# A hybrid encoder layer on one core: the last 256 gate and up columns as one unit of seven block products, S5's chain paced anew, and an idle product ahead of the keys

## The chip, the cores and the metric

The kernel runs on one core of a Trainium2 chip. The metric is the time of one execution on the device in microseconds, as a median of several runs. Beside it stands one profiled execution, with its own time and a trace of every instruction.

## The reference

The layer takes 512 tokens of width 1024 in float32. Cut to what matters:

```python
n = rms_norm(h, mix_norm_g)
proj = n @ w_in                                   # 1024 -> 512 + 4 * 1024
xa, zu, zv = ...                                  # S5 input, gating inputs
gate_a, gate_b = sigmoid(...), sigmoid(...)
ya = s5_branch(xa, ...)                           # two diagonal recurrences, forward and backward, GLU
yb = gelu(zu) * (w_s @ layer_norm(gelu(zv)) + bias)   # 128-token chunks, 8 heads
h = h + (gate_a * (ya @ w_proj_a) + gate_b * (yb @ w_proj_b)) @ w_out
h = h + cross_attention(rms_norm(h), rms_norm(mem))   # 256 memory tokens, 4 heads
f = rms_norm(h, ffn_norm_g)
h = h + (silu(f @ w_gate) * (f @ w_up)) @ w_down      # 1024 -> 2816 -> 1024
return rms_norm(h, final_norm_g)
```

## The kernel before, in words

Every large product keeps nearly the accuracy of float32: an operand is split into a high part (a cast on ScalarE, line 85) and a remainder (a subtraction on VectorE, line 86), and a product is three matmuls, high x high, high x low, low x high (`mm3`). TensorE reads the parts, so each weight block of 512 KB costs a load, a cast and a subtraction. `plan` lists all weight blocks in the order of their use; `next_w` issues the loads of the next ones and splits the next two (`SPLITS`); the parts rotate through three buffers, `hi` and `lo`.

The queries, the gate and up products and the down product save one product in eight: with both operands cut into 2 x 2 blocks, seven products of sums of blocks stand for the eight (Strassen's scheme in Winograd's form). A **unit** is 512 columns of a gate or up matrix. Its seven products are numbered 1 to 7; each takes a weight block `b11`, `b21`, `b22` or a sum `t` of blocks, against a block of the token matrix `fn` or a sum of such blocks (`ops`). The tokens are cut into T0 and T1 (256 each), the 1024 rows into K0 and K1. Products 1 and 2 need only T0; product 5 needs the first token sum (`sum1`: T1 rows of K0 minus T1 rows of K1), 6 and 7 the next ones (`sum2`), 3 the last (`sum4`). A product is 24 matmuls of 256 columns (`product`, line 1331). The block sums of the weights are made by an adding DMA on GpSimd's queue (line 181) and by VectorE (line 184). The pool `stp[0]` holds two buffers each of `t`, `b21` and `b22`; `b11` lies in the three raw buffers.

The inner width is 2816 = 5 x 512 + 256. The ten units (gate and up, five times 512 columns) are followed by the down product. The last 256 columns of gate and up (from `FS` = 2560 on) are plain products, four blocks of gate and four of up, which run first, with products 1 and 2 of unit 0 between the gate blocks. Under them the last token tile's norm, its transposes and the token sums are made. `begun` holds the started next unit; each unit's loop runs 5, 6, then 1 of the next unit, 7, 2 of the next unit, 4, 3. `put` writes the activation: SiLU for gate, a multiplication for up. `pair` holds the result of the last 256 columns.

`long_idle` is a matmul of 512 columns whose result nobody reads. Two stand in the kernel: behind the last token tile's transposes ahead of the feed-forward part (`behind=ot_hi`), and behind product 5 of unit 0.

Ahead of this runs the mixing stage. The S5 branch is a side program, a Python generator that `tick` drives while the large products run: `tick(us)` gives it `us * side["rate"]` of credit, and each `yield` takes some. `later(n, f)` calls `f` after n steps, a step being 5.2 us of ticks. Per octet of groups `s5_kernels` makes the factors `e` on VectorE, the block-diagonal tiles `bd` (two memsets on GpSimd, four copies on ScalarE), the products `pk`, and then stores, spills to DRAM and loads the kernels `tt` (16 small DMAs on GpSimd's queue). `pump` applies one ready set of input weights per half step (`pz`). `s5_scan` is the recurrence on VectorE, four small instructions a step. `s5_outputs` mixes (`py`), applies gelu (`squash`), turns back (`back`, `pyt`) and writes out. The gating loop (`psv`, line 1092) evacuates eight heads on VectorE (line 1093).

The order of each engine's instructions is settled when the program is built, from program order and a model of durations, as `schedule_with_timeline_sim=True` says; only instructions marked `in_order` keep theirs. So the trace's order is not always that of the text.

Of the kernel before, what the change touches and what calls it, by code (L numbers as in the profile page):

```python
# [17 lines left out]
P = 128  # L18
# [34 lines left out]
def hybrid_layer_kernel(  # L53
# [108 lines left out]
    def plan_unit(w, c0, ordered=False):  # L162

        kh = KD // 2
        b = lambda i, j: block(w, i * kh, kh, c0 + 256 * j, 256)
        r = {}

        def fresh(nm):
            r[nm] = (wp if nm == "b11" else stp[0]).tile([P, kh, 256], F32, tag="raw" if nm == "b11" else nm,
                                                         name=nm, bufs=3 if nm == "b11" else 2)  # L170
            return r[nm]

        def plain(nm, src):
            def f():
                ins = nc.sync.dma_start(fresh(nm), src)
                if ordered:
                    in_order(ins)
            return f

        def onto(nm, src):  # L180
            return lambda: nc.gpsimd.dma_start(r[nm], src, accum_op=ALU.add)

        def tt(o, x, y, op):
            nc.vector.tensor_tensor(r[o], r[x], r[y], op)
# [38 lines left out]
    def plan_units(units, down):  # L223


        made = [plan_unit(*u, ordered=i == 1) for i, u in enumerate(units)]
        for i in range(2):
            plan_block(w_gate, 4 * i, 4, FS, 256, place=i + 1)
            plan.append(made[0][i + 1])
        plan_feat(w_up, FS, KD)  # L230
        for i, m in enumerate(made):
            nx = made[i + 1] if i + 1 < len(made) else {}
            between = [nx[1]] if nx else down[:2]
            plan.extend([m[5], m[6]] + between + [m[7]] + ([nx[2]] if nx else []) + [m[4], m[3]])
        plan.extend(down[2:])
# [76 lines left out]
    FS = 2560  # L312
    UNITS = [(w, c0) for c0 in range(0, FS, 512) for w in (w_gate, w_up)]
    down_tokens, down_plan = [], []
# [454 lines left out]
    def s5_kernels(o):  # L769
# [3 lines left out]
        pr, pi = st["pe"]  # L773
        es = []
        for i in range(2):
# [12 lines left out]
        def products():  # L788
            bd = []
            for i in range(2):  # L790
                t = s5p.tile([P, GO, 2, C], F32, tag="bd", name="bd", bufs=2)
                nc.gpsimd.memset(t, 0.0)
                for d in range(2):
                    hf = slice(64 * d, 64 * d + 64)
                    nc.scalar.copy(t[hf, :, d, :], st["b"][i][hf, gs, :])
                bd.append(t)
            ps = aux("pk", (P, 2, P))
# [16 lines left out]
        def store(ps):  # L814
# [5 lines left out]
            V.tensor_tensor(ks[:, :, 0:C], ks[:, :, 0:C], dd, ALU.add)  # L820
            later(1, lambda: spill(ks))

        def spill(ks):
            kd = dp.tile([GO, C, 15, C], F32, name=f"kd{o}")
            for j in range(4):
                kdj = kd.rearrange("(q j) c l e -> j c q (l e)", j=4)[j]
                nc.gpsimd.dma_start(kdj[:, :, 7 * C:15 * C], ks[32 * j:32 * j + C])
                nc.gpsimd.dma_start(kdj[:, :, 0:7 * C], ks[32 * j + C:32 * j + 2 * C, :, 0:7 * C])
            later(2, lambda: load(kd))

# [41 lines left out]
    def pump():  # L872
        if "u" in st and ready:
            n, wt = ready.pop(0)
            apply(*SETS[n], wt)
            applied.append(n)
        if len(applied) < len(SETS):
            later(0.5, pump)
# [25 lines left out]
    def s5_outputs(o):  # L904
# [28 lines left out]
        def squash(ps):  # L933

            nc.scalar.activation(yt[:, 0], ps, AF.Gelu_apprx_tanh)
            later(0.5, back)

# [147 lines left out]


    gbc = gbcs[0]
    sv = slot("A", (P, H, T), F32, "sv")
    for h in range(H):
# [6 lines left out]
        tick(0.9)  # L1096

    yb_hi = slot("E", (P, KD, T), F32R, "yb_hi")
    yb_lo = slot("D", (P, KD, T), F32R, "yb_lo")
# [122 lines left out]
    for half in range(2):  # L1222
        tokm(w_out, half * 512, mg, KD, add_evac(half, 0, feat_norm(g_x, hn_hi, hn_lo, hfull, True)))

# [230 lines left out]

    def gate_evac(m, j, ps):
        nc.scalar.activation(pair[:, j, :], ps, AF.Silu)

    def up_evac(m, j, ps):
        nc.vector.tensor_tensor(pair[:, j, :], pair[:, j, :], ps, ALU.mult)  # L1460


    a11, a12, a21, a22 = full[:, K0, T0], full[:, K1, T0], full[:, K0, T1], full[:, K1, T1]
# [20 lines left out]

    def unit_start(u):
        x, v = unit_bank("px"), unit_bank("pv")
        product(x, u, 1, True, ops)
        nc.scalar.copy(v, x)
        return x, v

    def put(u, f, ts, src):
        dst = acts(u[1] // 512, f)[:, :, ts]
        if u[0] is w_gate:
# [9 lines left out]

    ps = [bank("pf0"), bank("pf1")]
    ws = []

    def gate_part(i, ts):
        if ts is T0:
            ws.append((4 * i,) + next_w(w_gate, 4 * i, 4, FS, 256))
        feat_block(ps, ws[i], fn, KD, 4, ts, ts is T0)  # L1510
        tick(2.7)

    gate_part(0, T0)
    begun = unit_start(UNITS[0])
    gate_part(1, T0)
    unit_second(UNITS[0], begun[1])
    for i in range(2):
        gate_part(i, T1)
    for j in range(2):
        gate_evac(FS // P + j, j, ps[j])  # L1520
    sum1()
    later(1, sum2)
    feat(w_up, FS, fn, KD, up_evac, parts=2, ps=[aux("pf0"), aux("pf1")])
    V.tensor_tensor(pair[:, 0, T1], pair[:, 0, T1], pair[:, 1, T1], ALU.subtract)

# [44 lines left out]
    for i, u in enumerate(UNITS):  # L1570
        final = i == len(UNITS) - 1
        x, v = begun
        q = unit_bank("pq")
# [10 lines left out]
        nc.scalar.copy(u2, x)  # L1584
        if not final:
            begun = unit_start(UNITS[i + 1])
        else:
# [6 lines left out]
        if not final:  # L1594
# [141 lines left out]
```

## Time and profile before

| | us |
|---|---|
| median of 3 runs | 887.28 (887.0 to 889.22) |
| profiled execution | 885.71 |
| its span, first to last instruction | 883.9 |
| TensorE busy | 867.2 |
| VectorE busy | 623.7 |
| ScalarE busy | 477.8 |
| GpSimd busy | 99.6 |

The page's shares are shares of the span. PE is TensorE, PEld its weight loads, DVE VectorE, ACT ScalarE, POOL GpSimd, SPq the queue of the engine that issues most loads. The chain of waits gives start, length and what the time went to; a timeline row gives start, length, engine, line, operation, output and inputs, and in brackets the idle time ahead of it with what ended it. The mean granted clock of TensorE is 0.997.

### The profile page before, as it was taken

The page shows a single profiled execution, that of the slowest core. Times are in us where ns is not written, and L with a number is a line of the kernel's source. Part 1 is how long each engine was busy: PE and PEld are TensorE (multiplying, and loading weights), DVE is VectorE, ACT ScalarE, POOL GpSimd, SP SyncE. Part 2 cuts the span into 40 slices and gives each one's busy share as a digit, 9 for nine tenths or more (in the row PEclk, how much of TensorE's full clock was granted, in tenths as well). Part 3 has the DMA queues.
Part 4 walks back from the last instruction along what each step waited for, and adds up shares of the span by engine and source line. Part 5 has one row for each costly group of instructions (what it writes and reads, how often), then busy time and mean ns, then how long its engine had stood idle before and what let it go on. Part 6 is the DMA issues. An engine that isn't in the chain of part 4 may idle for free.

```text
span 883.9 us, 14489 instructions
## 1 busy us (share of the span) xinstructions
PE 867.2 (98%) x5625; PEld 765.1 (87%) x5625; DVE 623.7 (71%) x1020; ACT 477.8 (54%) x702; POOL 99.6 (11%) x162
## 2 busy tenths in 40 slices
PE   9999999999989999999999999999999999999996
PEld 6788888888768888889899878999999999888875
DVE  5699718997542367659757746767877768899875
ACT  6644887245754343548556535545445555556663
POOL 1001045100063010110000001101110110000000
PEclk9999999999999999999999999999999999999999
DMA  9449368975278777925678235536799963256672
GB/s 267 140 108 260 86 167 221 252 183 142 64 182 230 197 237 195 289 84 166 204 226 253 72 102 157 147 101 174 193 216 211 232 164 95 72 168 202 191 246 87
DMA packets 112134, 154.33 MB, mean 175 GB/s; under 512 B 13545, under 2 KB 78593, under 8 KB 112002
## 3 DMA queue, kind: packets, MB, share of 16 engines
q1 hardware_dynamic: 93042, 128.27, 45.8%
q0 software_dynamic: 16432, 24.09, 16.9%
q10 hardware_dynamic: 2592, 1.05, 0.5%
q8 instruction: 44, 0.72, 0.3%
q14 instruction: 24, 0.20, 0.1%
HBM read 146.60 MB, written 38.24 MB: 209 GB/s over the span
## 4 chain that ended last, share of the span: by engine, by line
PE 86%; ACT 5%; DVE 4%; DMA 3%; issue 2%; SPq 1%; POOLq 0%; POOL 0%; ACTq 0%; DVEq 0%
PE pf L350 24%; PE pt L350 16%; PE px L1331 12%; PE dx L350 7%; PE pq L1331 6%; PE dq L350 3%; PE pv L1331 3%; PE qx L1331 2%; PE dv L350 2%; PE po L350 1%; PE qq L1331 1%; DMA xt<-in_x_dram 1%; PE ptr L511 1%; PE pz L884 1%; ACT ss L916 1%
## 5 line engine op out<-in xcount | busy, mean ns | idle before, releaser
L86 DVE TENSOR_TENSOR wlo<-wraw,whi 128x1024 fp32r<-128x1024 f32 (+1 forms) x139 | 165.0, 1187 | 103.3 <-ACT whi L85 98.0
L85 ACT CAST whi<-wraw 128x1024 fp32r<-128x1024 f32 (+1 forms) x139 | 142.3, 1024 | 157.0 <-PE pf L350 43.0
L350 PE MATMUL pf<-xn,whi 128*128 128x512 f32 x448 | 139.9, 392 | 0.0
L350 PEld LDWEIGHTS pf<-xn,whi 128*128 128x128 f32 x448 | 83.5, 188 | 17.4 <-issue 0.5
L350 PE MATMUL pf<-xn,wlo 128*128 128x512 f32 x224 | 87.6, 391 | 0.0
L1331 PE MATMUL px<-fn,whi 128*128 128x256 f32 x480 | 83.3, 276 | 0.0
L1331 PEld LDWEIGHTS px<-fn,whi 128*128 128x128 f32 x480 | 72.4, 188 | 0.3 <-ACT u L1591 0.2
L85 ACT CAST whi<-b 128x1024 fp32r<-128x1024 f32 x40 | 42.1, 1054 | 50.3 <-PE px L1331 27.1
L86 DVE TENSOR_TENSOR wlo<-b,whi 128x1024 fp32r<-128x1024 f32 x40 | 48.9, 1223 | 27.1 <-ACT whi L85 27.1
L1331 PE MATMUL px<-fn,wlo 128*128 128x256 f32 x240 | 66.4, 277 | 0.0
L350 PE MATMUL dx<-whi,s 128*128 128x512 f32 x170 | 53.9, 392 | 1.4 <-ACT whi L85 1.0
L1331 PE MATMUL pq<-s,whi 128*128 128x256 f32 x320 | 55.1, 276 | 0.0
L85 ACT CAST whi<-t 128x1024 fp32r<-128x1024 f32 x30 | 31.6, 1054 | 36.1 <-PE pv L1331 12.9
L86 DVE TENSOR_TENSOR wlo<-t,whi 128x1024 fp32r<-128x1024 f32 x30 | 36.7, 1225 | 19.9 <-ACT whi L85 19.9
L350 PEld LDWEIGHTS pf<-xn,wlo 128*128 128x128 f32 x224 | 42.1, 188 | 8.9 <-issue 0.2
L1331 PEld LDWEIGHTS pq<-s,whi 128*128 128x128 f32 x320 | 48.2, 188 | 0.1
L1331 PEld LDWEIGHTS px<-fn,wlo 128*128 128x128 f32 x240 | 45.1, 188 | 0.0
L1331 PE MATMUL pq<-s,wlo 128*128 128x256 f32 x160 | 44.2, 277 | 0.0
L350 PE MATMUL pt<-whi,xn 128*128 128x512 f32 x128 | 42.7, 407 | 0.0
L350 PEld LDWEIGHTS dx<-whi,s 128*128 128x128 f32 x170 | 31.7, 188 | 8.5 <-ACT whi L85 1.2
L350 PE MATMUL dx<-wlo,s 128*128 128x512 f32 x85 | 33.2, 391 | 0.0
L1331 PEld LDWEIGHTS pq<-s,wlo 128*128 128x128 f32 x160 | 30.1, 188 | 0.0
(422 smaller groups left out, 2159.8 us busy)
## 6 DMA issues: line engine op xcount, KB each, us to landing
wraw<-in_w_in_dram SPq DMA_DIRECT2D x36, 512.0 KB, 5.0
dsum<-in_w_down_dram SPq DMA_DIRECT2D x20, 512.0 KB, 6.7
wraw<-dsum SPq DMA_DIRECT2D x20, 512.0 KB, 3.7
b<-in_w_gate_dram SPq DMA_DIRECT2D x15, 512.0 KB, 3.9
b<-in_w_up_dram SPq DMA_DIRECT2D x15, 512.0 KB, 5.4
wraw<-in_w_down_dram SPq DMA_DIRECT2D x15, 512.0 KB, 3.9
dsum<-in_w_down_dram POOLq DMA_DIRECT2D x10, 512.0 KB, 7.3
dsum<-dsum POOLq DMA_DIRECT2D x10, 512.0 KB, 7.2
```

Source lines behind the costliest of these rows:

```text
L85: hi = nc.scalar.copy(dst_hi, src)
L86: lo = nc.vector.tensor_tensor(dst_lo, src, dst_hi.bitcast(F32), ALU.subtract)
L350: nc.tensor.matmul(ps, a[x], b[y], start=start and i == 0, stop=stop and i == 2, skip_group_check=free)
L511: tr = nc.tensor.transpose(ps[:, j, :], src[:, k * P:(k + 1) * P], ident)
L884: nc.tensor.matmul(ps[:, g, :], wt[:, g, :], st["u"][:, o * GO + g, :], start=True, stop=True)
L916: nc.scalar.copy(s[lo_, :, 1:NCH], zv[lo_, :, 0:NCH - 1])
L1331: nc.tensor.matmul(ps[:, j, :], a[x], b[y], start=start and j == k == i == 0, stop=k == 3 and i == 2, skip_group_check=True)
```

## The change

1. The last 256 columns of gate and up become one unit of seven products, with gate as the first block column and up as the second. It is the first of eleven units. The eight plain products and their evacuations go.
2. Products 1 and 2 of the first two units and product 1 of the third are run ahead of the loop; product 2 of the third stands between products 6 and 7 of the first. `sum1` and `sum2` follow directly, not a step apart. From the third unit on, the loop is as before.
3. In S5, the `bd` tiles are made ahead of the factors `e` instead of with the products; the spill comes after half a step and the load after one (one and two before); the turn back one step after the gelu (half before); `pump` applies up to two sets at a time; during the gating loop the side program's rate is 0.3 instead of 0.8.
4. The transposes of the last token tile ahead of the attention keep program order, and an idle product on `mg_hi` follows them.

```diff
@@ plan_unit
-        b = lambda i, j: block(w, i * kh, kh, c0 + 256 * j, 256)
+        b = (lambda i, j: block((w_gate, w_up)[j], i * kh, kh, FS, 256)) if c0 == FS else \
+            lambda i, j: block(w, i * kh, kh, c0 + 256 * j, 256)
@@ plan_units
-        for i in range(2):
-            plan_block(w_gate, 4 * i, 4, FS, 256, place=i + 1)
-            plan.append(made[0][i + 1])
-        plan_feat(w_up, FS, KD)
+        plan.extend([made[i][q] for i in range(2) for q in (1, 2)] + [made[2][1]])
...
-            plan.extend([m[5], m[6]] + between + [m[7]] + ([nx[2]] if nx else []) + [m[4], m[3]])
+            if i < 2:
+                plan.extend([m[5], m[6]] + ([made[2][2]] if i == 0 else []) + [m[7], m[4], m[3]])
+            else:
+                plan.extend([m[5], m[6]] + between + [m[7]] + ([nx[2]] if nx else []) + [m[4], m[3]])
...
-    UNITS = [(w, c0) for c0 in range(0, FS, 512) for w in (w_gate, w_up)]
+    UNITS = [(w_gate, FS)] + [(w, c0) for c0 in range(0, FS, 512) for w in (w_gate, w_up)]
@@ s5_kernels: the loop that makes bd moves from products() to the start
-            later(1, lambda: spill(ks))
+            later(0.5, lambda: spill(ks))
-            later(2, lambda: load(kd))
+            later(1, lambda: load(kd))
@@ pump
-        if "u" in st and ready:
-            n, wt = ready.pop(0)
...
+        for _ in range(2):
+            if "u" in st and ready:
...
@@ squash
-            later(0.5, back)
+            later(1, back)
@@ the gating loop
+    side["rate"] = 0.3
...
+    side["rate"] = RATE
@@ w_out
-        tokm(w_out, half * 512, mg, KD, add_evac(half, 0, feat_norm(g_x, hn_hi, hn_lo, hfull, True)))
+        tokm(w_out, half * 512, mg, KD, add_evac(half, 0, feat_norm(g_x, hn_hi, hn_lo, hfull, True, behind=mg_hi)))
@@ put
+        if u[1] == FS:
+            dst = pair[:, :, ts]
+            if f == 0 and ts is T0:
+                nc.scalar.activation(dst, src, AF.Silu)
+            else:
+                if f == 0:
+                    t = np_.tile([P, 2, 256], F32, tag="ev", name="gate", bufs=2)
+                    nc.scalar.activation(t, src, AF.Silu)
+                    src = t
+                nc.vector.tensor_tensor(dst, dst, src, ALU.mult)
+            return
@@ ahead of the loop
-    gate_part(0, T0)
-    begun = unit_start(UNITS[0])
-    gate_part(1, T0)
-    unit_second(UNITS[0], begun[1])
...
-    sum1()
-    later(1, sum2)
-    feat(w_up, FS, fn, KD, up_evac, parts=2, ps=[aux("pf0"), aux("pf1")])
-    V.tensor_tensor(pair[:, 0, T1], pair[:, 0, T1], pair[:, 1, T1], ALU.subtract)
+    starts = []
+    for u in UNITS[:2]:
+        starts.append(unit_start(u))
+        unit_second(u, starts[-1][1])
+    starts.append(unit_start(UNITS[2], lambda name: aux(name, (P, 2, 256))))
+    sum1()
+    sum2()
@@ the loop over units
-        x, v = begun
+        x, v = begun if i > 2 else starts[i]
...
+        if i == 0:
+            unit_second(UNITS[2], starts[2][1])
...
-        V.tensor_tensor(u3, q, u3, ALU.subtract)
-        put(u, 1, T1, u3)
+        if i == 0:
+            V.tensor_tensor(pair[:, :, T1], q, u3, ALU.subtract)
+        else:
+            V.tensor_tensor(u3, q, u3, ALU.subtract)
+            put(u, 1, T1, u3)
...
+        elif i == 0:
+            V.tensor_tensor(pair[:, 0, T1], pair[:, 0, T1], pair[:, 1, T1], ALU.subtract)
```

More of the change, by code (lines that the diff above doesn't have):

```diff
@@ L773, in s5_kernels @@
         pr, pi = st["pe"]
-        es = []
+        es, bd = [], []
+        for i in range(2):
+            t = s5p.tile([P, GO, 2, C], F32, tag="bd", name="bd", bufs=2)
+            nc.gpsimd.memset(t, 0.0)
+            for d in range(2):
+                hf = slice(64 * d, 64 * d + 64)
+                nc.scalar.copy(t[hf, :, d, :], st["b"][i][hf, gs, :])
+            bd.append(t)
         for i in range(2):
@@ L788, in products @@
         def products():
[L789 to L796, printed above, removed]
             ps = aux("pk", (P, 2, P))
@@ L872, in pump @@
     def pump():
-        if "u" in st and ready:
-            n, wt = ready.pop(0)
-            apply(*SETS[n], wt)
-            applied.append(n)
+        for _ in range(2):
+            if "u" in st and ready:
+                n, wt = ready.pop(0)
+                apply(*SETS[n], wt)
+                applied.append(n)
         if len(applied) < len(SETS):
@@ L1454, in acts @@
         return rest[0][:, 2 * f:2 * f + 2, :]
[L1456 to L1460, printed above, removed]
     a11, a12, a21, a22 = full[:, K0, T0], full[:, K1, T0], full[:, K0, T1], full[:, K1, T1]
@@ L1483, in hybrid_layer_kernel, with unit_start @@
     ops = {1: fn_q(K0, T0), 2: fn_q(K1, T0), 7: fn_q(K0, T1), 4: fn_q(K1, T1)}
-    def unit_start(u):
-        x, v = unit_bank("px"), unit_bank("pv")
+    def unit_start(u, place=unit_bank):
+        x, v = place("px"), place("pv")
         product(x, u, 1, True, ops)
@@ L1500, in unit_second @@
         put(u, 0, T0, v)
[L1504 to L1511, printed above, removed]
-    gate_part(0, T0)
-    begun = unit_start(UNITS[0])
-    gate_part(1, T0)
-    unit_second(UNITS[0], begun[1])
[L1517 to L1520, printed above, removed]
+    starts = []
[3 more added lines that the diff above has]
+    starts.append(unit_start(UNITS[2], lambda name: aux(name, (P, 2, 256))))
     sum1()
-    later(1, sum2)
-    feat(w_up, FS, fn, KD, up_evac, parts=2, ps=[aux("pf0"), aux("pf1")])
-    V.tensor_tensor(pair[:, 0, T1], pair[:, 0, T1], pair[:, 1, T1], ALU.subtract)
+    sum2()
     made, last_job = {}, []
@@ L1584, in hybrid_layer_kernel @@
         nc.scalar.copy(u2, x)
-        if not final:
+        if 1 < i and not final:
             begun = unit_start(UNITS[i + 1])
-        else:
+        elif final:
             dx = [bank(f"dx{t}") for t in range(2)]
             down_product(dx, 1, True, range(2))
+        if i == 0:
+            unit_second(UNITS[2], starts[2][1])
         product(x, u, 7, False, ops)
@@ L1593, in hybrid_layer_kernel @@
             sum4()
-        if not final:
+        if 1 < i and not final:
             unit_second(UNITS[i + 1], begun[1])
-        V.tensor_tensor(u3, q, u3, ALU.subtract)
-        put(u, 1, T1, u3)
+        if i == 0:
[3 more added lines that the diff above has]
+            put(u, 1, T1, u3)
         product(x, u, 4, False, ops)
```

## The prediction

> **What bounds the kernel now.** I read the page's busy shares and its chain by engine first, then the chain of waits of the stretches that the change touches.
>
> ```profile
> span 883.9 us, 14489 instructions
> ...
> PE 867.2 (98%) x5625; PEld 765.1 (87%) x5625; DVE 623.7 (71%) x1020; ACT 477.8 (54%) x702; POOL 99.6 (11%) x162
> ...
> PE 86%; ACT 5%; DVE 4%; DMA 3%; issue 2%; SPq 1%; POOLq 0%; POOL 0%; ACTq 0%; DVEq 0%
> ```
>
> TensorE carries 86% of the chain that ends last, so there are only two ways to save time: fewer or shorter products, or fewer moments in which TensorE waits. The waits of PE, as who waited for whom, show how little there is of the second kind; these three lie in the S5 and gating stretch:
>
> ```profile
> PE pk L802 <- DVE e L785: 1.6, 1, 1.6
> PE pyt L941 <- ACT tt L935: 1.1, 1, 1.1
> ...
> PE psv L1092 <- DVE sv L1093: 0.9, 1, 0.9
> ```
>
> The chain, cut to the start of the feed-forward part, gives the price of a block product (24 matmuls of 256 columns):
>
> ```profile
> 564.51 0.23 PE long L503
> ...
> 566.86 16.96 PE pf L350 x144
> 583.82 2.83 PE pq L1331 x24
> 586.65 0.23 PE long L503
> ...
> 595.06 2.72 PE pv L1331 x24
> ```
>
> Two prices stand here: 16.96/6 = 2.83 us before the idle product at 586.65, and 2.72 us behind it. TensorE streams without a break in both. Why it has two paces the trace does not say; I only count with them.
>
> **Part 1: seven products for eight.** Before, the last 256 gate and up columns are 4 + 4 block products and the ten full units 7 each; from the first gate product to the third product of unit 0 there are 17, of which 11 (the eight, 1 and 2 of unit 0, its 5) lie ahead of the idle product at 2.83 and 6 behind it. After, the stretch has 16: six ahead (1, 2, 1, 2, 1 of three units, then 5) and ten behind. 11 x 2.827 + 6 x 2.72 = 47.42 us against 6 x 2.827 + 10 x 2.72 = 44.16: **-3.25 us**, on the path in full, since TensorE is never idle here.
>
> It is paid for elsewhere: 7 weight blocks are split instead of 4 (a cast on ACT and a subtraction on DVE each), three block sums are added on DVE, and two intermediate results are copied and subtracted. The eight plain products were the cover under which the fourth token tile's norm and the token sums were made. After, five products stand ahead of product 5, which needs the first sum. DVE and ACT before, as timelines:
>
> ```profile
> 564.86 1.22 DVE L1470 TENSOR_TENSOR full<-full 128x1024 f32<-128x1024 f32 x1 [0.65 <-ACT full L517]
> 568.19 1.22 DVE L86 TENSOR_TENSOR wlo<-t,whi 128x1024 fp32r<-128x1024 f32 x1 [2.10 <-ACT whi L85]
> 569.45 1.22 DVE L184 TENSOR_TENSOR t<-t,b 128x1024 f32<-128x1024 f32 x1
> 570.70 1.23 DVE L184 TENSOR_TENSOR b<-t,b 128x1024 f32<-128x1024 f32 x1
> 571.85 1.22 DVE L86 TENSOR_TENSOR s<-full,s 128x1024 fp32r<-128x1024 f32 x1
> ...
> 576.63 2.43 DVE L86 TENSOR_TENSOR s<-full,s 128x1024 fp32r<-128x1024 f32 x2
> ```
> ```profile
> 567.10 1.05 ACT L85 CAST whi<-t 128x1024 fp32r<-128x1024 f32 x1 [2.27 <-PE pv L1331]
> 568.17 1.28 ACT L1494 ACT_TABLE_LOAD   x1
> 569.47 0.60 ACT L1494 ACTIVATE a_up<-pv 128x512 f32<-128x512 f32 x1
> 569.96 1.04 ACT L85 CAST s<-full 128x1024 fp32r<-128x1024 f32 x1
> ```
>
> The fourth product ends at 566.86, a fifth at 569.69. The sum's subtraction ends at 566.08; with its cast (1.05) and remainder (1.22) right behind it the operand stands at 568.35: no wait. In the order of this trace, behind one weight split and two block sums on DVE, it stands at 573.07: 3.4 us of wait. Before, nobody noticed, as product 5 came at 583.82. The second sum's remainder ends at 577.85; product 5, begun at 573.07, ends at 575.9, so product 6 waits another 1.95. Bounds 0 and 5.35. The trace has its order from a program in which the sums are written down before those block sums, and still DVE took the block sums first; after, the sums come later in the program, which speaks for the upper end. That the product of the third unit can be drawn ahead speaks for the lower. I take half, **+2.5 us**.
>
> The table load moves ahead by two products (the first activation follows the first unit's product 2) and stays one load, 1.28 us with the activation 0.02 us behind it. The Trainium skill (ScalarE: Activation LUTs, "What ACT_TABLE_LOAD costs") gives about 2.66 us for a switch, its drain included; this trace shows no drain. By that figure ACT would hold the fourth tile's casts 1.4 us longer, and my estimate of the sum would be 1.4 us higher; the measured 1.28 us decides.
>
> Loads: four plain 512 KB loads on SP's queue go; five of the new unit come, one of them an adding one on POOL's queue, whose instructions wait there for descriptors and whose nearest consumer (the fifth split) is five products off. I cost them at nothing; the cover is those products. One load is different. The units' second blocks have two buffers, and the third unit's must wait until DVE has made unit 0's last block sum:
>
> ```profile
> b<-in_w_up_dram SPq DMA_DIRECT2D x15, 512.0 KB, 5.4
> ...
> tt<-kd POOLq DMA_DIRECT2D x32, 64.0 KB, 6.0
> ```
>
> (The second row is S5's, for part 2.) With the DVE order above the add ends at 570.70 + 1.23 + 1.22 = 573.15, the block lands at 578.6 and is split by 580.8; product 6 ends at 577.85 + 2.72 = 580.6. So it just fits, and what queues behind it on SP (the next units' loads) is wanted later still.
>
> **Part 2: S5's pacing.** Around the two waits at 248 and 256 us:
>
> ```profile
> 247.33 0.61 ACT L795 COPY bd<-bbr 64x128 f32<-64x128 f32 x2 [6.71 <-POOL bd L792]
> 247.94 0.60 ACT L795 COPY bd<-bbi 64x128 f32<-64x128 f32 x2
> 248.57 0.60 ACT L935 ACTIVATE tt<-py 128x512 f32<-128x512 f32 x1
> ...
> 253.60 1.05 ACT L85 CAST whi<-wraw 128x1024 fp32r<-128x1024 f32 x1
> ```
> ```profile
> 245.80 1.14 POOL L268 DMA_DIRECT2D dsum<-in_w_down_dram  x1 [18.66 <-DMA dsum<-in_w_down_dram]
> ```
> ```profile
> 254.68 1.22 DVE L86 TENSOR_TENSOR wlo<-wraw,whi 128x1024 fp32r<-128x1024 f32 x1 [7.18 <-ACT whi L85]
> ...
> 255.93 1.22 DVE L785 SCALAR_TENSOR_TENSOR e<-e,etmp 128x1024 f32<-128x1024 f32 x1
> ```
>
> ACT stood 6.71 us on the memset of the block-diagonal tiles, which stood on POOL behind an adding DMA; then came the four copies (1.21 us) and the gelu for which the turn back waited 1.1. With the tiles built ahead of the e products, that block leaves; with the turn a full step after the gelu, the 1.1 goes. The copies behind it, the cast at 253.60, the split and e move up by the same 1.21, so of the 1.6 for e about 1.2 goes. The rate of 0.3 in the gating loop lets 8 x 0.9 x 0.3 / 0.8 = 2.7 recurrence steps through instead of 7, so the 0.9 for sv goes: together **-3.2 us** (bounds 0 and -3.6). Late next would be the recurrence, some 4 steps later, and the turn, half a step more for each of four octets; against that stand the doubled pump ahead of the recurrence and the spill and load of the kernels, 1.5 steps (7.8 us) earlier. The end has room:
>
> ```profile
> L350 PE MATMUL pf<-yg_hi,whi x16: 389/389/389, 315.9 to 326.1; 128*128 128x512 f32 x16
> ...
> L86 DVE TENSOR_TENSOR yg_lo<-ygt,yg_hi x4: 684/688/692, 306.4 to 308.5; 128x512 fp32r<-128x512 f32 x4
> ```
>
> S5's last operand is split by 309.2 and wanted from 315.9. Inside, however, the mixing products are placed right where the kernel's blocks land: the loads take 6.0 us each, and if products are drawn earlier than the loads can follow, TensorE waits. I add **+0.3 us** for new waits of that kind, bounds 0 and 3.6 (all that was won).
>
> **Part 3: idle product ahead of the keys.** Keys and values run at the slow pace too:
>
> ```profile
> 409.00 10.96 PE pf L350 x93
> 419.96 22.40 PE pt L350 x96
> ...
> 785.81 14.96 PE dq L350 x66
> ```
>
> 93 matmuls at 117.8 ns against 113.3 (2.72/24) are 0.42 us, 96 at 233.3 against 226.7 (14.96/66) are 0.64. One idle product costs 0.23. If it changes the pace: -0.83; if not: +0.23. Of the two idle products that the trace has, the one at 564.51 changed nothing and that at 586.65 did. Half: **-0.3 us**.
>
> **The sum.** -3.25 + 2.5 - 3.2 + 0.3 - 0.3 = -3.95 us against the profiled execution's own 885.71 us (span 883.9 and 1.8 around it): 881.8. That execution lies 1.57 under the median of the runs shown, 887.28, so the forecast for a median is 883.3 us.
>
> **The rivals.**
> *All covered.* The first sum is split at once, the third unit's product fills what is left, the pace of the keys changes: -3.25 - 3.6 - 0.83 = -7.7, 879.6 us. For it: DVE stood idle for 2.10 us ahead of 568.19.
> *Given back.* DVE keeps the order shown and the start costs its full 5.35, so the unit ends 2.1 behind; S5 still gains 3.2 and the rest is level: 886.2 us, not to be told from no change. For it: the DVE rows above, word for word.
> *Slower: the third unit's second block.* If the last block sum of unit 0 slips behind the token sums on DVE, it ends at 577.85 + 1.22 = 579.1, the block lands at 584.5 and is split by 586.8, while product 6 ends at 580.6: TensorE waits 6.2 us more if that product stands in its queue ahead of product 7. The start then costs 11.5, net +8.3; with S5's -3.2 it is +5.1, 892.4 us. It decides once the add ends behind 573. Against it: the add is written down ahead of the sums.
> The trace has the price of a cold TensorE as well:
>
> ```profile
> 1.06 4.22 PE L544 MATMUL idle<-ones 128*128 128x128 f32 x20 [1.06 <-DVE dcol L748]
> ```
>
> That is 211 ns a product at the kernel's start, ahead of which the engine had stood still. The Trainium skill (TensorE: Matmul & The Clock Gate, Part 1) says that an idle window of some 3.4 us halves the clock for as long again; by that rule, a 6.2 us wait would cost about 1.7 us more and this rival would stand at 894.1. No wait in this trace is long enough to show it.
>
> **How the numbers follow.** Forecast 0.55, all covered 0.15, given back 0.18, slower 0.12. The measurement tells about 0.3% (2.7 us) from no change, so faster means under 884.6 and slower over 889.9. The forecast's own range is 880.5 to 886 (2.7 either way at the start alone), some 0.47 of its 0.55 under 884.6. Faster: 0.15 + 0.47 = 0.62; same: 0.18 + 0.08 = 0.26; slower 0.12. The range, 879.3 to 888.8, holds the first three cases and leaves the slower one and slips of the first out. Most of the chance is of one sign.
>
> **What would show it.** The products pf from fn and s are gone, px, pv and pq stand at 11 units; the stretch from the first unit's product to unit 0's third is 44.2 us plus its waits. A wait of PE pq for DVE s is the step I priced at 2.5; a wait of pv for whi or wlo of a block b just behind it is the slower rival. The waits pyt and pk and psv are gone or small; py waiting for a DMA of tt would be my 0.3 gone wrong. The keys show 113 ns or 118 ns a matmul. I am wrong if the time lies over 886 with no such wait, or if a new wait stands in a part that I cost at nothing.

## The result: 12 us slower, and the profile after

| | before | after |
|---|---|---|
| median (4 runs each, same chip) | 888.25 (887.0 to 889.6) | 900.2 (898.16 to 901.15) |
| profiled execution / its span | 885.71 / 883.9 | 901.15 / 899.4 |
| mean granted clock | 0.997 | 0.989 |

The ratio is 1.0131, with an interval of 1.0106 to 1.0157. I had forecast 883.3 us (879.3 to 888.8). The two profiled executions lie 15.4 us apart, more than the medians; some 2 us of that is not the change's (below).

The page after: TensorE's share of the chain that ends last has dropped from 86 to 84%, and VectorE's and ScalarE's have risen.

```profile
span 899.4 us, 14461 instructions
...
PE 872.0 (97%) x5602; PEld 767.8 (85%) x5602; DVE 631.4 (70%) x1028; ACT 484.6 (54%) x710; POOL 100.9 (11%) x163
...
PE 84%; ACT 6%; DVE 5%; DMA 3%; issue 2%; SPq 0%; POOLq 0%; POOL 0%; ACTq 0%; DVEq 0%
```

The waits of PE after (waiter, releaser, us in total, times, longest):

```profile
PE pq L1334 <- ACT s L85: 5.5, 1, 5.5
PE pq L1334 <- ACT whi L85: 2.0, 2, 1.0
...
PE px L1334 <- ACT s L85: 1.7, 1, 1.7
PE px L1334 <- ACT u L1577: 1.5, 1, 1.5
PE psv L1094 <- DVE sv L1095: 1.5, 2, 0.8
...
PE pk L802 <- DVE e L793: 0.8, 1, 0.8
```

Four rows are new in the feed-forward part, 10.7 us in all: product 5 of the first unit waits for the first token sum (5.5), the first matmul of product 6 for the second (1.7), and TensorE waits at three places in the first two units (2.0 and 1.5). The row for the turn back (pyt) is gone, that of pk halved, that of psv grown.

The chain of waits after, from the end of the products that run ahead (start, length, what), with one product from behind the wait:

```profile
570.54 1.22 DVE t L185
...
574.63 1.14 DVE wlo L86
575.76 1.14 DVE full L1466
576.90 1.13 DVE t L185
578.03 1.15 DVE full L1471
...
579.20 1.05 ACT s L85
...
580.88 4.91 PE pq L1334 x23
...
586.48 2.71 PE px L1334 x23
```

For 10 us the chain runs along VectorE: block sums (L185), remainders (L86) and token sums (L1466, L1471) one behind the other. Then product 5 takes 4.91 us for 23 matmuls, 213 ns each, and product 6 behind it 2.71. The second wait is put down to product 6, but product 5's second matmul reads the remainder of the first sum, which VectorE made behind a block sum and the second token sum:

```profile
579.09 1.22 DVE L86 TENSOR_TENSOR s<-full,s 128x1024 fp32r<-128x1024 f32 x1
```

It ended at 580.31, when the wait ended too, so product 5 could not have gone on earlier in any case. ScalarE's timeline shows what the first sum (L1466) had to wait for:

```profile
572.75 0.58 ACT L518 COPY full<-ptr 128x512 f32<-128x512 f32 x1
...
576.93 1.04 ACT L85 CAST s<-full 128x1024 fp32r<-128x1024 f32 x1 [3.12 <-DVE full L1466]
```

The copy of the last half tile, which ended at 564.8 before, ends at 573.33 now. Its transposes had ended at 567.6; ahead of it on ScalarE stand the table load (567.00), two activations (568.29 and 569.73) and two casts, of a token sum (570.66) and of a weight block (571.80). VectorE then makes two remainders (573.41 to 575.77) before it turns to the sum.

How full VectorE is: busy time of the engines and the granted clock in windows of 5 us, first before, then after (columns: window, length, PE, PEld, DVE, ACT, POOL, PEclk, DMA share, GB/s).

```profile
570.00:575.00 5.00, 5.00 (x45) 5.00 (x44) 4.93 (x5) 2.20 (x4) 0.00 (x0) 1.00 0.01 1
575.00:580.00 5.00, 5.00 (x44) 5.00 (x44) 4.03 (x4) 2.10 (x2) 0.00 (x0) 1.00 0.00 0
580.00:585.00 5.00, 5.00 (x45) 5.00 (x44) 3.00 (x4) 3.06 (x3) 0.00 (x0) 1.00 0.01 3
```
```profile
570.00:575.00 5.00, 2.52 (x22) 2.31 (x20) 5.00 (x6) 3.43 (x5) 0.00 (x0) 1.00 0.00 0
575.00:580.00 5.00, 0.58 (x1) 0.29 (x1) 5.00 (x5) 1.84 (x2) 0.00 (x0) 0.59 0.47 122
580.00:585.00 5.00, 4.70 (x22) 4.70 (x23) 4.53 (x5) 2.25 (x3) 0.98 (x1) 0.50 0.89 297
```

Before, VectorE is busy for 12.0 of 15 us while TensorE streams; after, for 14.5 of 15, while TensorE stands for 7.2 of them, and the clock falls to half.

### The profile page after: what moved, and what is told of

The parts are those of the page before. It is cut to its first block, busy times and chain, and to the rows that moved or that the text cites. A ratio compares the mean times of both kernels' runs of the same rounds, so it can differ in the third digit from the quotient of the medians.

```text
span 899.4 us, 14461 instructions
## 1 busy us (share of the span) xinstructions
PE 872.0 (97%) x5602; PEld 767.8 (85%) x5602; DVE 631.4 (70%) x1028; ACT 484.6 (54%) x710; POOL 100.9 (11%) x163
## 3 DMA queue, kind: packets, MB, share of 16 engines
q10 hardware_dynamic: 2592, 1.05, 0.5%
## 4 chain that ended last, share of the span: by engine, by line
PE 84%; ACT 6%; DVE 5%; DMA 3%; issue 2%; SPq 0%; POOLq 0%; POOL 0%; ACTq 0%; DVEq 0%
PE pf L351 22%; PE pt L351 16%; PE px L1334 13%; PE pq L1334 7%; PE dx L351 6%; PE dq L351 3%; PE pv L1334 3%; PE qx L1334 2%; PE dv L351 2%; PE po L351 1%; PE qq L1334 1%; DVE wlo L86 1%; ACT whi L85 1%; PE ptr L512 1%; PE py L930 1%
## 5 line engine op out<-in xcount | busy, mean ns | idle before, releaser
L86 DVE TENSOR_TENSOR wlo<-wraw,whi 128x1024 fp32r<-128x1024 f32 (+1 forms) x137 | 162.4, 1186 | 117.8 <-ACT whi L85 117.2
L1334 PE MATMUL px<-fn,whi 128*128 128x256 f32 x528 | 92.4, 278 | 1.5 <-ACT u L1577 1.5
L1334 PEld LDWEIGHTS px<-fn,whi 128*128 128x128 f32 x528 | 79.8, 188 | 2.6 <-ACT u L1577 1.7
L85 ACT CAST whi<-b 128x1024 fp32r<-128x1024 f32 x44 | 46.4, 1054 | 53.9 <-PE px L1334 25.8
L86 DVE TENSOR_TENSOR wlo<-b,whi 128x1024 fp32r<-128x1024 f32 x44 | 53.8, 1222 | 28.6 <-ACT whi L85 28.6
L1334 PE MATMUL px<-fn,wlo 128*128 128x256 f32 x264 | 73.1, 277 | 0.0
L1334 PE MATMUL pq<-s,whi 128*128 128x256 f32 x352 | 63.5, 284 | 7.6 <-ACT s L85 5.5
L1334 PEld LDWEIGHTS pq<-s,whi 128*128 128x128 f32 x352 | 55.0, 194 | 8.2 <-ACT s L85 5.7
L86 DVE TENSOR_TENSOR wlo<-t,whi 128x1024 fp32r<-128x1024 f32 x33 | 40.4, 1224 | 22.1 <-ACT whi L85 22.1
L1334 PEld LDWEIGHTS px<-fn,wlo 128*128 128x128 f32 x264 | 49.7, 188 | 0.0
L1334 PE MATMUL pq<-s,wlo 128*128 128x256 f32 x176 | 49.5, 283 | 0.0
L1334 PEld LDWEIGHTS pq<-s,wlo 128*128 128x128 f32 x176 | 34.1, 195 | 0.0
```

The source lines that it names most:

```text
L85: hi = nc.scalar.copy(dst_hi, src)
L86: lo = nc.vector.tensor_tensor(dst_lo, src, dst_hi.bitcast(F32), ALU.subtract)
L1334: nc.tensor.matmul(ps[:, j, :], a[x], b[y], start=start and j == k == i == 0, stop=k == 3 and i == 2, skip_group_check=True)
```

## The experiments

The theories: **order** (the token sums are late because of where they stand on ScalarE and VectorE), **banks** (the third unit, begun early, holds two of three auxiliary PSUM banks, so the last transposes come late), **clock** (a wait costs TensorE its clock on top), **cover** (units without a neighbour's product between their own have bare places, where TensorE waits), **work** (VectorE's operations do not fit under the shortened cover, in any order).

### Halving the change: ffn_only and rest_only

ffn_only is before with edits 1 and 2 alone, rest_only with 3 and 4 alone.

> The kernel before with only the change of the feed-forward part (edits 1 and 2). From the two traces I read the loss as 13 us in this part, of which 7.9 us are two waits of TensorE for the first token sums (5.7 and 2.2), 2.2 us a fifth product at half clock, 4.1 us three short waits in the first two units, less the 2.7 us of the product saved and with small change. If the loss sits here alone: 900 to 903 us, with the same waits in the trace. If S5 or the keys carry part of it, or the parts get in each other's way: under 898 us.

> The kernel before with only S5's new pacing and the idle product ahead of the keys (edits 3 and 4). By the trace of the changed kernel: the wait of 1.1 us for the turn gone, that for e down from 1.6 to 0.8, those for sv up by 0.6 to 1, the idle product +0.25 and no change of the keys' pace: 1 to 2 us faster than before, 886 to 887.5 us. My prediction had -3.2 and -0.3 for these: 884.8 us. If the startup of the changed kernel, 3 us longer in its trace, belongs to the edits: 889 us or more.

ffn_only took 899.18 us against 888.31, ratio 1.0129 (1.0104 to 1.0153); rest_only 886.68, ratio 0.9983 (0.9968 to 0.9998). The loss is the feed-forward part's, 10.9 us by the medians, a little under what I expected; the rest gains 1.6, as expected. The halves add to 9.3 us where the whole lost 12.0 (9.4 to 13.9 by its interval): 0.8 us of that is a slower pace (below), and the rest lies within the intervals. In rest_only the wait for sv is still there, and VectorE's timeline shows what it is for:

```profile
163.26 0.75 DVE L1094 SCALAR_TENSOR_TENSOR sv<-psv,gbc,mix 128x512 f32<-128x512 f32 x1
163.92 1.22 DVE L86 TENSOR_TENSOR wlo<-wraw,whi 128x1024 fp32r<-128x1024 f32 x1
165.05 0.22 DVE L900 TENSOR_TENSOR sa<-sa,zh 128x64 f32<-128x64 f32 x1
165.19 1.40 DVE L1094 SCALAR_TENSOR_TENSOR sv<-psv,gbc,mix 128x512 f32<-128x512 f32 x2
```

Between the first two evacuations stand a weight remainder of 1.22 us and a single instruction of the recurrence, 0.22 us. The rate does not move the remainder.

**s5_only** drops the rate and the keys' idle product from rest_only.

> The kernel before with S5's new pacing only (factors and tiles, spill, load, pump, turn), without the lower rate in the gating loop and without the idle product ahead of the keys. The trace of rest_only has the pyt wait gone and half of that for e (-2.1 us), the idle product at +0.25 and two waits for sv (1.3 us against 1.1), both behind a weight remainder of 1.22 us on VectorE, which the rate does not touch. So 0 to 0.5 us faster than rest_only: 886.0 to 886.7 us. By my prediction's step for the rate it would be 0.9 us slower.

885.87 us, ratio 0.9985 (0.9971 to 0.9998): the rate buys nothing. These two are the versions that beat both kernels, by 1.3 to 1.6 us, just outside the noise.

### The wait's second price: warm

```diff
+    warm_ps = aux("warm")
+    for _ in range(22):
+        in_order(nc.tensor.matmul(warm_ps, fn_hi[:, 7, 384:512], fn_hi[:, 7, :], start=True, stop=True))
     sum1()
```

> The changed kernel with 22 idle products of 512 columns (22 x 0.23 = 5.1 us) on the last token tile ahead of product 5 of the first unit, where TensorE waits for 5.7 us. They leave every other engine as it is. Theory clock: the 4.91 us for 23 matmuls of product 5 (213 ns each) and the slower pace behind are the price of the wait itself; with TensorE kept busy product 5 takes 2.6 to 2.8 us: 2 to 3 us faster than the changed kernel, 897 to 898 us. If product 5 is slow for another reason (its operands, a port): the same time as the changed kernel, and 213 ns a matmul again.

896.1 us (895.41 to 896.53), ratio to before 1.0091 (1.0066 to 1.0115): 4.1 us under the changed kernel by the medians, 3.6 by the ratios, more than the 2 to 3 I expected. From warm's chain of waits:

```profile
578.59 2.71 PE pq L1334 x23
...
581.77 2.61 PE px L1334 x23
```

Product 5 takes 2.71 us instead of 4.91, with idle work ahead of it, so 2.2 us of the loss was the clock and not work. By the Trainium skill (TensorE: Matmul & The Clock Gate, Part 1) the cold array's matmuls start N / 1.2 GHz apart, N being the columns; an estimate from that is 213 ns for 256, and the trace of the changed kernel has 213. The products behind it run at 2.61 instead of 2.71 us for 23 matmuls, over seven products some 0.8 us. The wait for the sum itself is no shorter. 0.6 us is within the ranges.

### Order: copy_first, copy_b3

In `to_feat`, for the tiles of the feed-forward part, the copy `full` for the token sums comes ahead of the split instead of behind it (the edit put simply):

```diff
-            if q != skip:
-                split(hi[...], lo[...], ps)
             if full is not None:
                 nc.scalar.copy(full[...], ps)
+            if q != skip:
+                split(hi[...], lo[...], ps)
```

> The changed kernel, but ScalarE copies a token tile for the token sums before it casts it, not after (feed-forward part alone). Theory order: the first sum was late because this copy stood behind casts and activations of the units on ScalarE, and the sum behind block sums on VectorE. Then the copy ends some 4 us earlier, the waits of 5.7 and 2.2 us shrink to under 2 us together and the cold product goes with them: 8 to 10 us faster than the changed kernel, 890 to 892 us. Theory banks: the third unit's two auxiliary banks make the last transposes late (3.7 us between the two groups of four); then the copies cannot move ahead of them and the gain is 0 to 3 us, 897 to 900 us.

899.83 us, ratio 1.013 (1.0104 to 1.0157): nothing gained, and yet theory order was right about the first wait. The waits and the chain:

```profile
PE pv L1334 <- ACT whi L85: 2.9, 1, 2.9
...
PE px L1334 <- ACT s L85: 2.0, 1, 2.0
```
```profile
579.36 1.15 DVE t L185
...
580.52 3.67 DMA b<-in_w_up_dram
...
586.57 4.36 PE pv L1334 x22
```

The 5.5 us for the first sum are gone: it begins at 568.46 instead of 575.68, so the banks were not its cause. In their place stands my slower rival: the first unit's last block sum (L185) has slipped behind the token sums to 579.36, the load of the third unit's second block waits for its buffer, and product 2 waits for the load and runs cold. The rival had priced this wait at 6.2 us; it took 2.9, and 0.8 more for the remainder.

copy_b3 is copy_first with a buffer of its own for that block (a part of the activations' tile that is still empty).

```diff
+            if nm == "b21" and w is w_up and c0 == 0:
+                r[nm] = spare[0]          # a_lo_[:, 6:8, :]
+                return r[nm]
```

> As copy_first, and the second block of the third unit is loaded into a buffer of its own (a part of the tile for the later activations that is still empty) and so no longer waits for the first unit's last block sum. In copy_first the waits for the token sums shrank from 8.1 to 2.8 us, but the third unit's product 2 stood for 3.1 and 1.0 us for that block and ran 22 matmuls in 4.1 us: my prediction's slower rival, brought on by the token sums going first on VectorE. If the two compete through that buffer alone, these 4.2 us and the cold matmuls behind (1.5 us) go, and nothing else comes: 893 to 895 us. If VectorE's work is the bound in any order, another operand is late instead and the time stays at 898 to 900 us.

894.71 us, ratio 1.0067 (1.0049 to 1.0085): as expected from order, 5.1 us. What is left is a wait of 2.0 (for a copy that stands behind casts on ScalarE), a cold product 5 and the bare places:

```profile
PE px L1337 <- ACT u L1581: 3.1, 2, 1.5
PE pq L1337 <- ACT whi L85: 2.0, 2, 1.0
PE pv L1337 <- ACT pv L1488: 2.0, 1, 2.0
...
574.02 3.89 PE pq L1337 x23
```

### Cover: cover, copy_b3_cover, copy_b3_cover_pin

cover changes the order of products in the first units (those of other units in brackets):

```diff
-unit 0: 5, 6, [2 of unit 2], 7, 4, 3
-unit 1: 5, 6, 7, 4, 3
-unit 2: 5, 6, [1 of unit 3], 7, [2 of unit 3], 4, 3
+unit 0: 5, 6, [2 of unit 2], 7, [5 of unit 1], 4, 3
+unit 1: 6, [1 of unit 3], 7, [5 of unit 2], 4, 3
+unit 2: 6, [2 of unit 3], 7, [5 of unit 3], 4, 3
```

> The changed kernel, but product 5 of the second unit stands between 7 and 4 of the first, and products 5 of the third, 1 and 2 and 5 of the fourth between those of the second and third; from the fifth unit on as before. In the changed kernel the first two units have three bare places (1.3, 1.8 and 1.3 us), where the next product must wait until ScalarE has copied the accumulator. Theory cover: these 4.4 us less three quarters: 896.5 to 898 us. If the waits only move (to a weight block that is not split yet): 899 to 901 us.

894.21 us, ratio 1.0076 (1.0046 to 1.0107): 6.0 us under the changed kernel by the medians, 4.9 by the ratios. Of the new waits of PE only two are left:

```profile
PE pq L1335 <- ACT s L85: 5.5, 1, 5.5
PE px L1335 <- ACT s L85: 1.7, 1, 1.7
```

The bare places (3.5 us) are gone and the waits for the sums are as they were, so the covers did what theory cover says. The rest of the gain, more than I expected, is within both ranges (892.5 to 898.8 and 898.2 to 901.2).

> copy_b3 and cover together. If the causes are separate the gains add: 890 to 892 us. If they compete for the same splits on ScalarE and VectorE, less than 1 us more than copy_b3: 893 to 895 us.

894.42 us, ratio 1.0071 (1.0049 to 1.0094): nothing on top of copy_b3, so the gains did not add. In the profiled execution the reason is not the splits, as I had written, but the pace. Chains of no_idle (below), copy_b3_cover and before, one row each, 72 matmuls of 256 columns without a wait:

```profile
608.32 8.48 PE px L1331 x72
```
```profile
629.08 8.48 PE px L1338 x72
```
```profile
605.94 8.16 PE px L1331 x72
```

8.48/72 is 117.8 ns, 8.16/72 is 113.3. copy_b3_cover ran its units at 117.8 ns in this execution, from a wait near 583 to the end of the units; that costs about 0.32 per 72 matmuls, 7 us in all, and hid the gain. The pace of its other three executions is not on record.

copy_b3_cover_pin is copy_b3_cover with the first sum's cast kept ahead of the first activations (`in_order` on both).

> copy_b3_cover, and the cast and remainder of the first token sum keep program order ahead of the first two units' activations (with the table load) on ScalarE. In copy_first that cast came at 571.4 us, 1.8 us after its sum was ready, and the remainder 2.4 us after product 5 could have begun. If that order was the rest of the wait: 1.5 to 2.5 us faster than copy_b3_cover, 888 to 890 us. If the activations then come late themselves: no gain.

891.65 us (890.12 to 898.64), ratio 1.0038 (1.0024 to 1.0052): 2.8 us under copy_b3_cover, though short of the 888 to 890 I expected. The profiled execution, the 898.64, ran at 117.8 ns; 7 us less is where the other five lie, but only the profiled execution's trace is kept, so that they ran at 113 is inferred. The two profiled executions, both at 117.8 ns from 583 us on, say the opposite of the medians, 898.64 against 894.97; so the 2.8 us is not shown to be the order's.

### The pace: no_idle

```diff
             split(*fn_q(K0, T1), s3)
-            long_idle(fn_hi)
```

> The kernel before without the idle product behind product 5 of the first unit. In all traces so far the time from one matmul of 256 columns to the next is 113.3 or 117.7 ns, stays the same as long as TensorE streams, and changes only at a break (transposes, a wait, an idle product); copy_b3_cover ran its whole feed-forward part at 117.7 and so showed no gain from its covers. In the kernel before the step from 117.7 to 113.3 stands at that idle product. If the pace is kept from break to break and nothing else sets it: the units run at 117.7 ns to their end, 68 products x 24 x 4.4 ns = 7.2 us, so 894 to 896 us. If the pace comes from the operands or from the loads that run beside: 113 ns as before, 888 us.

893.93 us against 887.15, ratio 1.0072 (1.0059 to 1.0085): 6.8 us (7.2 expected) for one idle product of 0.23 left out, and the row of 8.48 above. The pace is kept from one break to the next, and one break decides over 170 us. Which way a break turns it I can't say: the idle product of the changed kernel ahead of the keys turned nothing (shown under part 3), and in copy_b3_cover_pin the one behind product 5 turned it to the slow side. A third case, from sfi_nosum (next section), has the idle product in the middle of an unbroken stream:

```profile
663.17 5.65 PE pq L1339 x48
668.83 0.23 PE long L509
669.06 8.18 PE px L1339 x72
```

That is 117.7 ns a matmul ahead of it and 113.6 behind it, with no wait between.

### Work: sum_first, sum_first_idle, and VectorE relieved

sum_first is copy_b3_cover with the first sum written ahead of the third unit's first product; this sum's split, the weight splits written with that product and the first activations keep program order. sum_first_idle adds an idle product behind product 5 of the sixth unit. Against the changed kernel, cut to this place:

```diff
     for u in UNITS[:2]:
         starts.append(unit_start(u))
-        unit_second(u, starts[-1][1])
+        product(starts[-1][1], u, 2, False, ops)
+    pinned[0] = True
+    sum1()
     starts.append(unit_start(UNITS[2], ...))
-    sum1()
+    for u, (_, v) in zip(UNITS, starts[:2]):
+        put(u, 0, T0, v)
+    pinned[0] = False
     sum2()
```

> copy_b3_cover, and the first token sum is written ahead of the third unit's first product, with its cast and remainder and the splits behind it kept in program order, the first two units' activations after them. In copy_b3_cover_pin the cast still stood 4.5 us behind its subtraction (573.0 against 568.4 us), behind the splits of the next blocks. If VectorE's and ScalarE's order is the rest of the loss: product 5 starts without a wait and at full clock, 4 to 5 us less than copy_b3_cover_pin at the same pace: 886 to 888 us at 113 ns, 893 to 895 us at 118 ns. If the work itself does not fit under five products: products 6 or 2 of the third unit wait instead, 889 to 891 us at 113 ns.

> sum_first with one more idle product of 512 columns, behind product 5 of the sixth unit. If sum_first runs its units at 118 ns and an idle product can change that: 4 to 5 us faster than sum_first. If it runs them at 113 ns: the same or, if the idle product changes the pace the other way, 4 to 5 us slower. If an idle product changes nothing: +0.2 us.

sum_first took 898.26 us (890.58 to 900.54), ratio 1.0104 (1.0073 to 1.0135), its trace at 117.8 ns; sum_first_idle 892.64 (891.34 to 894.05), ratio 1.0061 (1.0044 to 1.0079), at 113.3 ns already 80 us ahead of the added idle product. So that product is not shown to have done anything in this trace; the pace fell differently at the waits. In both, product 5 starts without a wait, and others wait instead (sum_first_idle):

```profile
PE px L1338 <- DVE s L86: 2.0, 1, 2.0
PE long L508 <- ACT fn L85: 1.6, 1, 1.6
...
580.62 5.28 PE px L1338 x23
```

Three orders of the same work (the changed kernel, copy_first, sum_first), three different late operands; in sum_first_idle VectorE is busy for all 20 us from 565 to 585. That speaks for work. But the second of these rows is ScalarE's: the cast it names stands at 572.93 behind the table load and both activations, and ScalarE is busy for 4.97 of the 5 us from 570 to 575. To test it, after_nosum and sfi_nosum are without the weight-block sums of the first three units on VectorE; after_pool and sfi_pool make them on GpSimd.

```diff
-            nc.vector.tensor_tensor(r[o], r[x], r[y], op)
+            (nc.gpsimd if c0 in (FS, 0) else nc.vector).tensor_tensor(r[o], r[x], r[y], op)   # pool
+            if c0 not in (FS, 0): ...                                                        # nosum
```

> The changed kernel without the sums of weight blocks on VectorE in the first three units (left out: three subtractions or additions of 1.22 us a unit, so that products 6, 7 and 4 of these units take wrong blocks). Three of them, 3.7 us, stand among the token sums between 570 and 578 us, and one of them holds back the load of the third unit's second block. Theory work (VectorE is busy without a break from 570 to 585 us and its work does not fit): the first sum comes 2.4 us earlier (the two block sums ahead of it), the second wait shrinks too, and with a shorter cold stretch 3 to 6 us are gained: 894 to 897 us. Theory order: as the sums could be done in time by another order alone, less than 1 us: 899 us or more.

> sum_first_idle without the same sums (left out as in after_nosum). There product 5 begins without a wait, but product 2 of the third unit, product 6 and product 5 of the second unit wait 1.9, 1.2 and 2.2 us, and 22 matmuls run in 4.9 us. Theory work: most of these 5.3 us and 2 us of the cold stretch go: 886 to 888 us. Theory order: the waits stay, 892 us.

> The changed kernel with these sums on GpSimd instead of VectorE. If GpSimd needs up to about 3 us for one and leaves VectorE alone: as after_nosum, 894 to 898 us. If it is much slower or holds VectorE up, the sums come later than before and so do products 6, 7 and 4: 900 us or more.

> sum_first_idle with these sums on GpSimd. If GpSimd is quick enough and leaves VectorE alone: as sfi_nosum, 886 to 889 us. If not: 893 us or more.

| | us | ratio to before |
|---|---|---|
| after_nosum | 895.51 | 1.0089 (1.0063 to 1.0116) |
| sfi_nosum | 889.31 | 1.0014 (0.9993 to 1.0034) |
| after_pool | 904.51 | 1.019 (1.0165 to 1.0216) |
| sfi_pool | 894.53 | 1.0076 (1.0047 to 1.0105) |

By the ratios the sums are worth 3.7 us in the changed kernel and 4.2 in sum_first_idle: the first as expected from work, the second less (its trace still has waits of 0.6, 0.9, 1.0 and 1.0 us and a partly cold product, and the slow pace up to the added idle product at 668.8 us). In after_nosum the third unit's second block also comes earlier, as its load no longer waits for a sum; in sfi_nosum that block has its own buffer, and the gain is as large, which speaks for VectorE's time. So VectorE's work is a cause, beside its order, and not the whole one. On GpSimd the sums lose time. GpSimd's sums in after_pool, grouped, and VectorE's groups of the same stretch (busy, mean ns):

```profile
L185 POOL TENSOR_TENSOR t<-t,b 128x1024 f32<-128x1024 f32 x6 | 16.0, 2674 | 14.5 <-DVE wlo L86 9.5 <-issue 5.0
...
L86 DVE TENSOR_TENSOR s<-full,s 128x1024 fp32r<-128x1024 f32 x1 | 3.4, 3369 | 0.0
...
L1470 DVE TENSOR_TENSOR s<-full 128x1024 f32<-128x1024 f32 x1 | 2.4, 2397 | 1.2 <-ACT full L518 1.2
```

A sum takes 2.7 us there, and VectorE operations that fall beside one take 3.4 and 2.4 us instead of 1.2. The one of 3.4 began 0.92 us into a sum of 3.21 and ended 1.1 us behind it: the two engines don't run side by side on such operands. The Trainium skill (SBUF — State Buffer, "SBUF: two separate sides") says so: a VectorE operation with two SBUF inputs and a GpSimd operation that reads SBUF take a pair of ports in turn, each for its whole length; the trace agrees.

## Why the prediction was wrong, point by point

**The step that failed** is the cost of the first sums, "half, +2.5 us" between "bounds 0 and 5.35". The rows measured 5.5 and 1.7, and 2.2 for the cold product: 9.4 us. The bounds were none: I took the order of the block sums from the trace of before and left everything upstream of the sum at before's times. But the copy that the sum needs ended 8.5 us later, behind the units' work on ScalarE, and VectorE had no room left. The sign that I had named was a wait for `DVE s`; the row reads `ACT s`, as the cast itself came late. I never added up VectorE's work under the shorter cover: it was busy for 12.0 of the 15 us from 570 to 585 already, and my own text counts three weight splits and three block sums more.

**Not priced at all:** the bare places, 3.5 us. My front text says that the loop is as before "from the third unit on", and I read past what that says of the first two: after product 6 or 7 the next product of the same unit waits for ScalarE's copy of the accumulator, as no neighbour's product stands between. At all three places ScalarE first casts a weight block (1.05 us), so the rows name that cast or the copy.

Together: -3.25 for the product saved, +9.4 and +3.5 make +9.7; ffn_only measured +10.9 (9.2 to 13.6 by its interval). In the changed kernel some 0.8 at the slow pace up to 607 us comes on top: the -3.25 had counted on the idle product behind product 5 to turn the pace, as before, and there it did not.

**The slower rival** did not occur in the changed kernel: product 2 of the third unit followed without such a wait. Its condition did: the add ended at 578.0, behind 573, and the load was issued at 578.06; but product 5 itself ran until 585.8, so TensorE did not have to wait for it. The mechanism was right, as copy_first shows with the add behind the token sums; the mark of 573 was wrong, as it took the sums' times from the trace of before. My chance of 0.12 for slower stood on one mechanism of several that share a cause.

**The clock.** I had the rule for a wait of 6.2 us in a rival alone, 1.7 us. The first wait of the main case, up to 3.4 in my own bounds, deserved it too.

**The table load**, at nothing beyond 1.28 us: it stands in the trace at 567.00 with 1.28 us and the activation 0.01 us behind it, without a drain. But it stands ahead of the last copies of the token tile, where before it stood behind them.

**Part 2**, -3.2 and +0.3: measured with part 3, -1.6. The pyt wait (1.1) went; that for e fell by 0.8, not 1.2; the 0.9 for sv stayed, since its cause was a weight remainder and not the recurrence. The trace of before has the same remainder in the same place, ahead of the second evacuation at 161.59 and of two instructions of the recurrence (0.22 us each):

```profile
160.19 1.22 DVE L86 TENSOR_TENSOR wlo<-wraw,whi 128x1024 fp32r<-128x1024 f32 x1
```

No new wait of py came, so the +0.3 was not needed.

**Part 3**, half between -0.83 and +0.23: the upper end. The keys and values after:

```profile
412.30 0.23 PE long L504
412.53 10.13 PE pf L351 x86
422.66 22.40 PE pt L351 x96
```

117.8 and 233.3 ns on both sides of the idle product, as before.

The values' stretch starts 2.7 us later than before (419.96). no_idle, whose program up to there is that of before, has it at

```profile
421.84 22.40 PE pt L350 x96
```

so 1.9 us of such a difference comes and goes with the execution.

**Range and chances.** 0.88 stood on faster or same; the range reached to 888.8. My four cases priced VectorE's order, none its load. What stays open: what turns the pace at a break, and whether some order of the start fits VectorE's and ScalarE's work (none of those tried did).

## What to carry to other kernels

When cover is taken from an engine that helps (here 28 us of products to 14), add up that engine's whole work in the stretch before asking which operation comes first; if it fills the stretch, reordering moves the wait to the next operand, as copy_first and sum_first did. Price a wait with what it does behind itself: here 7.2 us of waits brought 2.2 us at half clock. And look at the pace of the stream on both sides of every break before believing that two gains don't add.

## What the runs showed of the hardware that I had not expected

- Two paces of the same matmul stream, 113.3 and 117.8 ns for 256 columns, both at a granted clock of 1.00, kept until the next break; worth 6.8 us here. A single idle product turned it in before, in sfi_nosum (both to the fast side) and in copy_b3_cover_pin (to the slow side).
- Half clock after less of a wait than I had reckoned with: in copy_b3 a wait of 2.0 us, with a single matmul and 0.4 us of standing ahead of it, was enough for 23 matmuls in 3.89 us (2.61 at full clock).
- A GpSimd sum of 128x1024 takes 2.7 us on average and stretches VectorE's neighbouring operation from 1.2 to as much as 3.4 us.
